# Keys of a prompt turned by VectorE in blocks of 32 and stored from SBUF, buffers released at the last scores, output units 512 columns wide

## The chip, the cores and the metric

The kernel runs on one core of a Trainium2 chip. The metric is the device time of one execution in microseconds (us): the median of three runs was 294.86 us (294.21 to 295.25). The engines named below are PE (TensorE, matmuls), DVE (VectorE), ACT (ScalarE), POOL (GpSimd) and SP (SyncE, which issues nearly all transfers). SBUF is the on-chip memory in 128 partitions, PSUM the accumulators that PE writes, in eight banks of 128 x 512 floats. A DMA moves data between the chip's DRAM and SBUF.

## The reference

One decoder layer is computed for two groups: a prompt of 512 tokens and 8 decode tokens, each with its own past. All data is float32.

```
h = x @ w_in                      # (512 + 8) x 1024 by 1024 x 3600
qa, ka, va, za, ga, qb, kb, vb, gb = split(h)
o_a = gated linear attention(qa, ka, va, gate(za)), 4 heads, chunked, RMS-normalised
o_b = dilated attention(qb, kb, vb), 8 heads of 64; three patterns of distances, one merged softmax
mix = [o_a * silu(ga), o_b * silu(gb)]
y   = LayerNorm(2**0.25 * x + mix @ w_out)       # 1024 x 1024
outputs: y for both groups, the states of the linear attention,
         the keys kb and values vb of both groups, token by token
```

For this change one output matters most: `k_win_prompt`, the keys of the prompt, 512 tokens x 512 features (1 MB), with one row per token.

## The kernel before

**Layout.** The input x is held transposed (features on partitions, tokens on the free axis). A projection in the feature-major form (`feature`) multiplies a weight tile of 128 columns with x and yields 128 features on partitions and the tokens on the free axis, in two units: 264 columns (256 prompt tokens and the 8 decode tokens) and 256 columns. Every unit accumulates over 8 pieces of the contraction (KT = 8), and each piece takes three matmuls, because weights and x are each split into a high and a low part in the fast float32 format (`fp32r`): high x high, high x low, low x high. So a unit has 24 matmuls. Splitting is one copy on ACT (the high part) and one subtraction on DVE (the low part).

**Keys.** `kb` comes in four groups of 128 features (m = 0 to 3), each in two units (u = 0, 1). Its evacuation (`parts`) writes the high part on ACT and the low part on DVE into `kp{m}`, which the scores use. The output wants token-major keys. Before, `keys_token_major` does it at the very end: for each of four token tiles eight matmuls against an identity turn the high and low parts and add them in PSUM, ACT copies the result into SBUF (`keys_out`, line 1024), and a 256 KB store leaves, the first from SP and three from ACT. These copies wait for `rstd3`, a step of the last normalisation.

**Output projection.** `out_first` computes the first 256 tokens and the decode tokens in feature-major units (g, f) of 264 columns; each is turned back by PE (`out_turn`). `out_unit` then computes the token tiles t = 2 and 3 token-major, in units of 24 matmuls with 256 output columns: `wo` holds four groups of 256 columns. `out_evac` adds the unit to the residual rows `y{t}` on DVE and gathers the statistics of the LayerNorm; `norm(t)` finishes a tile and stores it, in two halves for t = 3.

**Order.** The order of the work is found by a planner when the program is built (`Plan`, lines 189 to 358). Each task is a generator with a priority. The planner models when each engine is free and when operands are ready, and takes the operation that can start first, the lower priority number first among equals. `At(name, n)` holds a task back until a mark was set n times in this planning; it is no wait on the chip. `Need(tag, ...)` takes a buffer slot from a pool and holds the task back while none is free; `free` returns it, after as many calls as `share` asked for. On the chip each engine executes its list in order and waits only where data or buffer reuse demand it. So SP, whose transfers have one queue, issues in the planned order, as early as the slots allow.

**Pools.** "g" has 27 slots of 4 KB per partition (projections, keys, queries, gates, mix tiles, output rows), "w" 6 for split weights, "r" 2 for raw weights, "t1" 4 and "t2" 3 for small things. Split pieces of w_out may also use slots of "sv", "pt" and "g" (`Group.part`). PSUM banks are "d" (3, projections), "s" (3) and "t" (2). Before, `weighted` returns the query tiles `qh`, `ql` after the last weighted sum of a half (line 1194), and the key tiles `kp` after the turns at the end (line 1198).

**The decode path.** The eight decode tokens have their own chain: POOL multiplies past keys with the queries, DVE reduces, a softmax follows, then POOL and DVE do the same with past values. Its results enter the first output units through `mix_sample`.

Of the kernel before, what the change touches and what calls it, by code (L numbers as in the profile page):

```python
# [75 lines left out]
class Op:  # L76
# [3 lines left out]
    def __init__(self, eng, fn, args, kw):  # L80
# [13 lines left out]
        if fn == "dma_start":  # L94
            c = 640 if eng.name == "SP" else 100
            x = aps[aps[0].tensor.space == bass.MemoryType.DRAM]
            run = 4 * min(run_of(x) for x in aps)

            rate = 175 if x.ap[0][1] <= 64 else 340 if run >= 4096 else 230
            self.xfer = max(4 * total(x) / rate, 200)  # L100
            self.late = 600 * (rate == 175)
        elif eng.name == "PE":
            m, n, slow = size(aps[1]), size(aps[2]), aps[2].dtype == F32

            self.mode = tuple(32 if x <= 32 else 64 if x <= 64 else P for x in (aps[1].ap[0][1], m if slow and fn != "transpose" else P))
# [83 lines left out]
class Plan:  # L189
# [18 lines left out]
    def mark(self, name):  # L208
        self.marks[name] += 1
# [152 lines left out]
def trunk(ctx: ExitStack, tc: tile.TileContext, xT, xp, xs, state, ck, cv, w_in, wab, gnorm,  # L362
# [54 lines left out]
    rb = cst("rb", [66, NB, HB], F32R)  # L417
    ident_r = cst("ident_r", [P, P], F32R)
    ka_s, qa_s = cst("ka_s", [P, 2, NB]), cst("qa_s", [P, 2, NB])
# [25 lines left out]
    class Group:  # L445


        def __init__(self, src, c0, name, width):
            self.src, self.c0, self.name, self.w = src, c0, name, width
            self.parts = 1 if width == P else 2  # L450
            self.kk = KT // self.parts
            self.hi, self.lo, self.tiles = [], [], []

        def load(self, i):
# [13 lines left out]
        def split(self, i, raw):  # L468
            a = yield from self.part(f"hi{i}_")
            b = yield from self.part(f"lo{i}_")  # L470
            self.tiles.append((a, b))
            n = self.kk // self.parts
# [16 lines left out]
    groups = {f"{n}{i}": w_group(n, i, w) for n, c, w in names for i in range(c)}  # L489
    wo = [Group(w_out, g * GW, f"wo{g}_", GW) for g in range(4)]  # L490
    order = [g for k, g in groups.items() if k != "ka0"] + wo
# [89 lines left out]
    def fills():  # L581
        yield V.memset(rb.bitcast(F32)[64:66], 1.0)
        yield At("const")
        yield S.copy(ident_r, ident)
        mark("ident_r")
        raw = B["rb_raw"]
# [29 lines left out]
    def token(g, evac_f, evac):  # L616

        for f in range(2):
            fs = slice(f * P, f * P + P)
            ps = yield bank("d", f"ps_{g.name}f{f}")  # L620
            for k in range(KT):
                yield At(g.name, k // 2 + 1)
                h, l = xh[k][:, TS[0]], xl[k][:, TS[0]]
# [11 lines left out]
    def turn(ps):  # L635
# [5 lines left out]
        for t in range(2):  # L641
            yield T.transpose(o[:, t * P:t * P + P], f[:, t * P:t * P + P], ident)
        free(f)
        return o

# [20 lines left out]
    def dense():  # L666
# [29 lines left out]
        for x in ("qh0", "ql0", "qh1", "ql1"):  # L696
            yield from make(x, Need("g", x, [P, 4, 256], F32R))
        for i in range(4):
            yield from feature(groups[f"qb{i}"], parts("q", q_s, i, 0.125))
        for i in range(4):  # L700
            yield from make(f"kp{i}", Need("g", f"kp{i}", [P, 2, 512], F32R))
            yield from feature(groups[f"kb{i}"], parts("k", k_s, i, 1.0))
# [19 lines left out]
        for x in units[3:]:  # L722
            yield from out_first(x)
        for t in range(2, 4):
            for g in range(4):
                yield from out_unit(t, g)
        for t in range(TT):
            yield from keys_token_major(t)

# [267 lines left out]
    def parts(n, own, m, scale):  # L997

        def evac(ps, u):
# [6 lines left out]
            if u == 0:  # L1006
                yield S.mul(own[:, m, :], ps[:, 256:TW[0]], scale)
            free(ps)
            mark(f"{n}b{m}{u}")
            mark(f"{n}b")  # L1010
        return evac

    def keys_token_major(t):
        for m in range(4):
            yield At(f"kb{m}{t // 2}")
        yield At("ident_r")
        ps = yield bank(("d", "s", "t"), "ps_kw")
        for m in range(4):
            for x in range(2):
                yield T.matmul(ps[:, m * P:m * P + P], B[f"kp{m}"][:, x, t * P:t * P + P], ident_r, start=x == 0, stop=x == 1)  # L1020
        mark("kw")
        add(keys_out(t, ps), 11)

    def keys_out(t, ps):
        yield At("rstd3")
        kw = yield Need("t2" if t % 2 else "st", "kw", [P, 512])
        yield S.copy(kw, ps)
        free(ps)
        yield (S if t else D).dma_start(kw_p[t * P:t * P + P, :], kw)
        free(kw)  # L1030

# [8 lines left out]
    def va_into(i):  # L1040
        def evac_f(ps, f):
            c = slice(i * GW + f * P, i * GW + f * P + P)
            yield copy(vat[:, 2 * i + f, :], ps[:, GW:TW[0]])
            mark("vat")
            ps = yield from turn(ps)
            yield copy(B["va0"][:, :, c], ps[:, :GW].rearrange("p (t c) -> p t c", t=2))
# [9 lines left out]
    def vb_into(i):  # L1056
# [4 lines left out]
        def evac_f(ps, f):  # L1061
            c = slice(i * GW + f * P, i * GW + f * P + P)
            yield copy(vnt[:, 2 * i + f, :], ps[:, GW:TW[0]])
            mark("vnt")
            ps = yield from turn(ps)
# [34 lines left out]
    def scores(m, pi, qt):  # L1100
# [12 lines left out]
        for u in range(pi + 1):  # L1113
# [54 lines left out]
    def weighted(h, pi):  # L1168
# [280 lines left out]

    def out_unit(t, g):  # L1450
        u, tl = t // 2, slice((t % 2) * P, (t % 2) * P + P)
        ps = yield bank("d", f"ps_y{t}{g}")
        for k in range(KT):
            yield At(wo[g].name, k // 2 + 1)
            yield At(f"mix_a{u}", t % 2 + 1) if k < 4 else At(f"mix_b{u}{k - 4}")
            mh, ml = (B[f"m{x}{'ab'[k // 4]}{u}"][:, k % 4, tl] for x in "hl")
            hi, lo = wo[g].hi[k], wo[g].lo[k]
            yield from three(ps[:, :GW], k, ((mh, hi), (mh, lo), (ml, hi)))
        add(out_evac(t, g, ps[:, :GW]), 2)

# [11 lines left out]
    def out_half(g, f, ps, ks):  # L1472
        fs = slice(f * P, f * P + P)
        for k in ks:
            yield At(wo[g].name, k // 2 + 1)
# [3 lines left out]
            hi, lo = wo[g].hi[k][:, fs], wo[g].lo[k][:, fs]  # L1479
            yield from three(ps[:, :TW[0]], k, ((hi, mh), (lo, mh), (hi, ml)))  # L1480
# [20 lines left out]
    def out_evac(t, g, ps):  # L1501
        yield At(f"y{t}")
        y, st = B["y", t], B["stats", t]
        c = slice(g * GW, g * GW + GW)
        yield V.scalar_tensor_tensor(y[:, c], y[:, c], ALPHA, ps, op0=ALU.mult, op1=ALU.add)
        free(ps)
        yield V.bn_stats(st[:, g, :], y[:, c])
        mark(f"y{t}_done")
        if plan.marks[f"y{t}_done"] == 4:
# [79 lines left out]
    add(mix_sample(), 16)  # L1589
    add(ln_rows(), 17)  # L1590
    for pi in range(2):
        for n in "ab":
# [106 lines left out]
```

## Time and profile before

| | |
|---|---|
| median of the runs | 294.86 us (294.21 to 295.25) |
| profiled execution, its own time | 296.48 us |
| span of the profiled execution | 294.7 us |
| PE busy | 282.2 us |
| DVE busy | 229.3 us |
| ACT busy | 165.3 us |
| DMA queue of SP, share of 16 engines | 60.1% |

The page gives for each engine its busy time in the span; a busy PE is a PE with a matmul under way, not one at its peak. A row of a timeline begins with the start and the duration in us; "x2" are two instructions merged, and a bracket at the end names idle time before it and what ended it. A row of the table by stages covers the window that it names. The line number L357 is that of a helper through which all instructions are issued, so groups are told apart by the names of their tiles. `ps_kb` are banks of the key projection, `ps_yf` those of the feature-major and `ps_y` those of the token-major output units, `ps_kw` those of the key turns.

### The profile page before, as it was taken

What the parts mean: (1) busy time and instruction counts of PE and PEld (TensorE: products, weight loads), DVE (VectorE), ACT (ScalarE), POOL (GpSimd) and SP (SyncE); (2) the same over time, 40 slices, a digit from 0 to 9 for tenths busy, and PEclk for the clock granted to TensorE, in tenths of its full rate; (3) what the DMA queues carried; (4) which work ended last, traced back from release to release, by engine and by line L of the source; (5) the groups of instructions that cost most, each with busy time, mean ns of one, the idle gap of its engine ahead of it and who ended that gap; (6) DMA issues with size and microseconds to landing.
All of it is one profiled execution on the core that took longest, in us unless ns stands there. A gap on an engine that the chain in (4) does not pass through costs nothing.

```text
span 294.7 us, 7011 instructions
## 1 busy us (share of the span) xinstructions
PE 282.2 (96%) x2696; PEld 268.5 (91%) x2696; DVE 229.3 (78%) x566; ACT 165.3 (56%) x454; POOL 55.6 (19%) x73
## 2 busy tenths in 40 slices
PE   6989999999999999899999999999999999999992
PEld 2979999998999999889899899998999999999992
DVE  3858377998879877887889976989889965349944
ACT  4768325554676757267659672769769854111003
POOL 3000000000195354300241449030320000000000
PEclk9999999999999999999999999999999999999996
DMA  7946432222887695635999989654964788100315
GB/s 189 325 119 202 125 98 73 76 71 76 246 316 222 177 308 186 177 97 155 268 207 181 218 211 285 166 143 144 281 166 137 233 274 318 40 0 27 122 73 214
DMA packets 54107, 51.20 MB, mean 174 GB/s; under 512 B 4116, under 2 KB 46904, under 8 KB 54074
## 3 DMA queue, kind: packets, MB, share of 16 engines
q1 hardware_dynamic: 53642, 49.97, 60.1%
q10 hardware_dynamic: 432, 0.79, 0.7%
q8 instruction: 21, 0.34, 0.5%
q14 instruction: 12, 0.10, 0.1%
HBM read 45.19 MB, written 6.03 MB: 174 GB/s over the span
## 4 chain that ended last, share of the span: by engine, by line
PE 23%; DVE 17%; DMA 7%; ACT 4%; issue 2%; POOL 1%; SPq 0%; DVEq 0%; POOLq 0%; ACTq 0%
PE ps_yf L357 8%; PE ps_y L357 8%; DMA pb<-psd_s 3%; DVE o_pv L357 2%; PE ps_va_f L357 2%; DVE oa L357 2%; ACT sg L357 2%; DVE gb L357 1%; DMA out_dram<-vb_raw 1%; DMA raw_gb__2786<-in_w_in_dram 1%; PE ps_va L357 1%; PE ps_pv L357 1%; DVE ga L357 1%; DMA s<-in_state_dram 1%; DVE y L357 1%
## 5 line engine op out<-in xcount | busy, mean ns | idle before, releaser
L357 POOL TENSOR_TENSOR vv<-vv,pb 128x256 f32<-128x256 f32 x32 | 26.2, 853 | 68.7 <-DMA pb<-psd_s 31.3
L357 POOL TENSOR_TENSOR past<-past,qbc 128x256 f32<-128x256 f32 x32 | 25.4, 827 | 42.0 <-DMA past<-in_ck_dram 39.1
L357 ACT ACTIVATE pr<-pr,ms 128x128 f32<-128x128 f32 (+3 forms) x43 | 23.2, 554 | 8.8 <-DVE ms L357 8.8
L357 PE MATMUL ps_pt<-cf,pr 128*128 128x128 f32 x80 | 14.0, 276 | 0.8 <-DVE pt L357 0.8
L357 DVE CUSTOM_DVE_ANT_0 pr<-ps_s,strip 128x128 f32<-128x128 f32 (+3 forms) x32 | 14.3, 480 | 0.6 <-PE ps_vb_f L357 0.6
L357 ACT ACTIVATE sg<-sg 128x264 f32<-128x264 f32 (+1 forms) x32 | 13.3, 417 | 0.4
L357 ACT COPY feat_y<-ps_yf 128x256 f32<-128x256 f32 x8 | 3.0, 373 | 17.1 <-PE ps_yf L357 17.1
L357 DVE TENSOR_TENSOR ptl<-ps_pt,pth 128x384 fp32r<-128x384 f32 (+1 forms) x16 | 9.6, 617 | 1.8 <-ACT pth L357 1.7
L357 ACT ACTIVATE rstd<-mv 128x1 f32<-128x1 f32 x4 | 0.7, 203 | 17.8 <-DVE mv L357 17.8
L357 DVE TENSOR_REDUCE o_pv<-vv 128x4 f32<-128x1024 f32 x8 | 9.7, 1214 | 1.0 <-POOL vv L357 1.0
L357 PEld LDWEIGHTS ps_pt<-cf,pr 128*128 128x128 f32 x80 | 9.2, 141 | 1.3 <-PE ps_vb_f L357 1.0
L357 POOL MEMSET att<- 64x512 f32 x2 | 1.0, 522 | 48.5 <-DVE ks L357 48.5
L357 ACT ACTIVATE sq<-oa 128x128 f32<-128x128 f32 x16 | 4.8, 301 | 9.3 <-DVE oa L357 9.1
L357 DVE TENSOR_REDUCE lt<-past 128x16 f32<-128x1024 f32 x8 | 9.6, 1204 | 0.0
L357 ACT CAST pth<-ps_pt 128x384 fp32r<-128x384 f32 (+1 forms) x16 | 8.3, 533 | 2.3 <-PE ps_pt L357 2.0
L357 DVE COPY lt<-ps_yf 128x8 f32<-128x8 f32 x6 | 1.0, 167 | 10.9 <-ACT feat_y L357 10.9
L357 ACT ACTIVATE d<-d 128x512 f32<-128x512 f32 x13 | 7.7, 637 | 3.0 <-DVE d L357 3.0
L357 DVE TENSOR_SCALAR pr<-pr,ms 128x256 f32<-128x256 f32 (+3 forms) x21 | 8.7, 428 | 0.2
L357 ACT CAST pt<-ps_pt 128x128 fp32r<-128x128 f32 (+1 forms) x16 | 5.1, 321 | 6.6 <-PE ps_pt L357 6.5
L357 ACT COPY pvl<-ps_pv 64x256 f32<-64x256 f32 x16 | 5.8, 370 | 5.3 <-PE ps_pv L357 3.2
L357 DVE TENSOR_TENSOR d<-b 128x1024 f32<-128x1024 f32 x7 | 8.5, 1219 | 0.0
L357 DVE TENSOR_TENSOR obT<-ps_pv,pvl 64x256 f32<-64x256 f32 x16 | 6.7, 416 | 2.4 <-ACT pvl L357 2.1
(551 smaller groups left out, 1155.4 us busy)
## 6 DMA issues: line engine op xcount, KB each, us to landing
past<-in_ck_dram SPq DMA_DIRECT2D x8, 512.0 KB
vv<-in_cv_dram SPq DMA_DIRECT2D x8, 512.0 KB
pb<-psd_s SPq DMA_DIRECT2D x16, 256.0 KB
qbc<-qsd SPq DMA_DIRECT2D x8, 256.0 KB
strip<-tabr SPq DMA_DIRECT2D x8, 256.0 KB
y<-in_xp_dram SPq DMA_DIRECT2D x4, 512.0 KB
x_raw<-in_xT_dram SPq DMA_DIRECT2D x7, 260.0 KB
out_dram<-y SPq DMA_DIRECT2D x3, 512.0 KB
```

The lines of the kernel that those rows point to most:

```text
L357: getattr(eng.eng, op.fn)(*op.args, **op.kw)
```

## The change

Keys: `keys_out` is now part of the evacuation of a key unit. After the high and low parts, DVE's 32x32 block transpose reads the unit's 256 columns out of PSUM and writes them to `kw{m // 2}`, a tile of pool "g"; only then is the bank returned. In each block of 32 x 32 tokens and features are swapped, so partition 32a + i holds token 32b + i and, at columns 32b to 32b + 31, the features 32a to 32a + 31. A new task `keys_store` (priority 17.5) issues 16 stores from SP once all turns are planned and the first output tile has its first evacuation: each takes 32 partitions and one m, 64 KB in runs of 32 floats. The matmuls against the identity, the identity in `fp32r`, the four copies and the four stores at the end are gone.

Buffers: `scores` returns `kp` and the two query tiles itself; queries are shared by four calls, keys by two.

Output: `wo` is two groups of 512 columns, each loaded in four pieces of two k (before: four groups in two pieces of four k), with one mark per k (`Group.at`). Token tile 2 has two units of 512 columns, tile 3 one of 512 and two of 256. The feature-major units pick their 128 columns out of the wider group.

Values: `turn` no longer returns its buffer; the turned values `vb` are copied back into it before their store.

```diff
-            rate = 175 if x.ap[0][1] <= 64 else 340 if run >= 4096 else 230
+            rate = 60 if run <= 128 else 175 if x.ap[0][1] <= 64 else 340 if run >= 4096 else 230
...
-    ident_r = cst("ident_r", [P, P], F32R)
...
-            self.parts = 1 if width == P else 2
+            self.parts = width // P
             self.kk = KT // self.parts
+            self.n = KT if width == P else 512 // width
...
+        def at(self, k):
+            return At(self.name, k // self.n + 1)
...
-    wo = [Group(w_out, g * GW, f"wo{g}_", GW) for g in range(4)]
+    wo = [Group(w_out, g * 512, f"wo{g}_", 512) for g in range(2)]
...
         for x in ("qh0", "ql0", "qh1", "ql1"):
-            yield from make(x, Need("g", x, [P, 4, 256], F32R))
+            yield from make(x, Need("g", x, [P, 4, 256], F32R), 4)
...
-            yield from make(f"kp{i}", Need("g", f"kp{i}", [P, 2, 512], F32R))
+            yield from make(f"kp{i}", Need("g", f"kp{i}", [P, 2, 512], F32R), 2)
...
-        for t in range(2, 4):
-            for g in range(4):
-                yield from out_unit(t, g)
-        for t in range(TT):
-            yield from keys_token_major(t)
+        for t, c, w in ((2, 0, 512), (2, 512, 512), (3, 0, 512), (3, 512, GW), (3, 768, GW)):
+            yield from out_unit(t, c, w)
...
+            if n == "k":
+                add(keys_out(ps, m, u), 2)
+            else:
+                free(ps)
...
-    def keys_token_major(t):
-        for m in range(4):
-            yield At(f"kb{m}{t // 2}")
-        yield At("ident_r")
-        ps = yield bank(("d", "s", "t"), "ps_kw")
-        for m in range(4):
-            for x in range(2):
-                yield T.matmul(ps[:, m * P:m * P + P], B[f"kp{m}"][:, x, t * P:t * P + P], ident_r, start=x == 0, stop=x == 1)
-        mark("kw")
-        add(keys_out(t, ps), 11)
-
-    def keys_out(t, ps):
-        yield At("rstd3")
-        kw = yield Need("t2" if t % 2 else "st", "kw", [P, 512])
-        yield S.copy(kw, ps)
-        free(ps)
-        yield (S if t else D).dma_start(kw_p[t * P:t * P + P, :], kw)
-        free(kw)
+    def keys_out(ps, m, u):
+        if m % 2 + u == 0:
+            yield from make(f"kw{m // 2}", Need("g", f"kw{m // 2}", [P, 2, NP]))
+        yield At(f"kw{m // 2}")
+        yield V.transpose(B[f"kw{m // 2}"][:, m % 2, u * 256:u * 256 + 256], ps[:, :256])
+        free(ps)
+        mark("kw")
+
+    def keys_store():
+        yield At("kw", 8)
+        yield At("y0_done", 1)
+        for i in range(2):
+            kw = B[f"kw{i}"].rearrange("p m (b j) -> p m b j", j=32)
+            for m in range(2):
+                for a in range(4):
+                    c = (2 * i + m) * P + a * 32
+                    yield D.dma_start(kw_p[:, c:c + 32].rearrange("(b i) j -> i b j", i=32), kw[a * 32:a * 32 + 32, m])
+            free(B[f"kw{i}"])
...
-            raw = yield Need("t1", "vb_raw", [P, GW])
             yield copy(raw, ps[:, :GW])
...
+        free(kp, *qx)
...
-            free(B[f"qh{pi}"], B[f"ql{pi}"])
             if pi:
                 free(*(B[f"vhl{i}{u}"] for i in range(2) for u in range(2)))
-                yield At("kw", TT)
-                free(*(B[f"kp{m}"] for m in range(4)))
...
-    def out_unit(t, g):
+    def out_unit(t, c, w):
...
-            yield from three(ps[:, :GW], k, ((mh, hi), (mh, lo), (ml, hi)))
+            hi, lo = g.hi[k][:, cs], g.lo[k][:, cs]
+            yield from three(ps[:, :w], k, ((mh, hi), (mh, lo), (ml, hi)))
...
+    add(keys_store(), 17.5)
```

More of the change, by code (lines that the diff above doesn't have):

```diff
@@ L471, in split @@
             self.tiles.append((a, b))
-            n = self.kk // self.parts
+            n = self.n
             for k in range(0, self.kk, n):
@@ L583, in fills @@
         yield At("const")
-        yield S.copy(ident_r, ident)
-        mark("ident_r")
         raw = B["rb_raw"]
@@ L621, in token @@
             for k in range(KT):
-                yield At(g.name, k // 2 + 1)
+                yield g.at(k)
                 h, l = xh[k][:, TS[0]], xl[k][:, TS[0]]
@@ L642, in turn @@
             yield T.transpose(o[:, t * P:t * P + P], f[:, t * P:t * P + P], ident)
-        free(f)
-        return o
+        return o, f
     def sample_rows(x, rows):
@@ L1007, in evac @@
                 yield S.mul(own[:, m, :], ps[:, 256:TW[0]], scale)
-            free(ps)
             mark(f"{n}b{m}{u}")
             mark(f"{n}b")
-        return evac
-    def keys_token_major(t):
-        for m in range(4):
-            yield At(f"kb{m}{t // 2}")
-        yield At("ident_r")
-        ps = yield bank(("d", "s", "t"), "ps_kw")
-        for m in range(4):
-            for x in range(2):
-                yield T.matmul(ps[:, m * P:m * P + P], B[f"kp{m}"][:, x, t * P:t * P + P], ident_r, start=x == 0, stop=x == 1)
-        mark("kw")
-        add(keys_out(t, ps), 11)
-    def keys_out(t, ps):
-        yield At("rstd3")
-        kw = yield Need("t2" if t % 2 else "st", "kw", [P, 512])
-        yield S.copy(kw, ps)
-        free(ps)
-        yield (S if t else D).dma_start(kw_p[t * P:t * P + P, :], kw)
-        free(kw)
+            if n == "k":
+                add(keys_out(ps, m, u), 2)
+            else:
+                free(ps)
+        return evac
+    def keys_out(ps, m, u):
[4 more added lines that the diff above has]
+        free(ps)
+        mark("kw")
+    def keys_store():
[8 more added lines that the diff above has]
+            free(B[f"kw{i}"])
     def sample_v(x, n, out):
@@ L1044, in evac_f @@
             mark("vat")
-            ps = yield from turn(ps)
+            ps, f_t = yield from turn(ps)
+            free(f_t)
             yield copy(B["va0"][:, :, c], ps[:, :GW].rearrange("p (t c) -> p t c", t=2))
@@ L1064, in evac_f @@
             mark("vnt")
-            ps = yield from turn(ps)
+            ps, raw = yield from turn(ps)
             yield from parts_of(B[f"vhl{i}0"][:, :, 2 * f:2 * f + 2], ps[:, :GW].rearrange("p (t h d) -> p t h d", t=2, d=64))
             mark(f"vb{i}0")
-            raw = yield Need("t1", "vb_raw", [P, GW])
             yield copy(raw, ps[:, :GW])
@@ L1448, in residual @@
         mark(f"y{t}")
-    def out_unit(t, g):
-        u, tl = t // 2, slice((t % 2) * P, (t % 2) * P + P)
-        ps = yield bank("d", f"ps_y{t}{g}")
+    def out_unit(t, c, w):
+        u, tl, cs = t // 2, slice((t % 2) * P, (t % 2) * P + P), slice(c % 512, c % 512 + w)
+        g = wo[c // 512]
+        ps = yield bank("d", f"ps_y{t}{c // GW}")
         for k in range(KT):
-            yield At(wo[g].name, k // 2 + 1)
+            yield g.at(k)
             yield At(f"mix_a{u}", t % 2 + 1) if k < 4 else At(f"mix_b{u}{k - 4}")
             mh, ml = (B[f"m{x}{'ab'[k // 4]}{u}"][:, k % 4, tl] for x in "hl")
-            hi, lo = wo[g].hi[k], wo[g].lo[k]
-            yield from three(ps[:, :GW], k, ((mh, hi), (mh, lo), (ml, hi)))
-        add(out_evac(t, g, ps[:, :GW]), 2)
+            hi, lo = g.hi[k][:, cs], g.lo[k][:, cs]
+            yield from three(ps[:, :w], k, ((mh, hi), (mh, lo), (ml, hi)))
+        add(out_evac(t, c // GW, ps[:, :w]), 2)
     def out_first(*units):
@@ L1472, in out_half @@
     def out_half(g, f, ps, ks):
-        fs = slice(f * P, f * P + P)
+        w, c = wo[g // 2], g % 2 * GW + f * P
         for k in ks:
-            yield At(wo[g].name, k // 2 + 1)
+            yield w.at(k)
             yield At("mix_a0", 2) if k < 4 else At(f"mix_b0{k - 4}")
@@ L1478, in out_half @@
             mh, ml = (B[f"m{x}{'ab'[k // 4]}0"][:, k % 4, :] for x in "hl")
-            hi, lo = wo[g].hi[k][:, fs], wo[g].lo[k][:, fs]
+            hi, lo = w.hi[k][:, c:c + P], w.lo[k][:, c:c + P]
             yield from three(ps[:, :TW[0]], k, ((hi, mh), (lo, mh), (hi, ml)))
@@ L1503, in out_evac @@
         y, st = B["y", t], B["stats", t]
-        c = slice(g * GW, g * GW + GW)
+        c = slice(g * GW, g * GW + size(ps))
         yield V.scalar_tensor_tensor(y[:, c], y[:, c], ALPHA, ps, op0=ALU.mult, op1=ALU.add)
         free(ps)
-        yield V.bn_stats(st[:, g, :], y[:, c])
-        mark(f"y{t}_done")
+        for i in range(g, g + size(ps) // GW):
+            yield V.bn_stats(st[:, i, :], y[:, i * GW:i * GW + GW])
+            mark(f"y{t}_done")
         if plan.marks[f"y{t}_done"] == 4:
```

## The prediction

> **What bounds the kernel now.** I read the page's busy times first, then what TensorE (PE) waited for, then a table of windows cut at the stages, and last the end of the chain of waits.
>
> ```profile
> span 294.7 us, 7011 instructions
> PE 282.2 (96%) x2696; PEld 268.5 (91%) x2696; DVE 229.3 (78%) x566; ACT 165.3 (56%) x454; POOL 55.6 (19%) x73
> ...
> PE ps_yf L357 <- ACT mha L357: 0.3, 1, 0.3
> ...
> 75.00:102.00 27.00, 27.00 (x239) 25.88 (x240) 23.12 (x74) 18.53 (x60) 15.47 (x20) 1.00 0.78 247
> 102.00:116.00 14.00, 13.63 (x117) 13.43 (x116) 10.37 (x32) 8.03 (x27) 5.65 (x8) 1.00 0.85 262
> 116.00:136.00 20.00, 18.65 (x153) 17.02 (x152) 16.52 (x44) 11.42 (x36) 4.29 (x4) 1.00 0.43 126
> ...
> 190.00:210.00 20.00, 19.02 (x157) 18.63 (x156) 18.09 (x54) 14.66 (x52) 2.84 (x4) 1.00 0.63 165
> ...
> 236.70:262.10 25.40, 25.37 (x208) 25.23 (x209) 11.78 (x32) 8.35 (x22) 0.00 (x0) 1.00 0.47 170
> 262.10:285.80 23.70, 23.70 (x201) 23.40 (x200) 18.16 (x55) 2.15 (x11) 0.00 (x0) 1.00 0.18 69
> 285.80:294.70 8.90, 3.67 (x34) 3.53 (x32) 4.64 (x12) 2.44 (x6) 0.00 (x0) 0.75 0.47 177
> ```
>
> In a window's row stand its length, then the busy us of PE, of weight loads, VectorE (DVE), ScalarE (ACT) and GpSimd, then clock, DMA share and GB/s. PE is busy all through 75 to 102 us and through the output projection (236.7 to 285.8), at full clock. Elsewhere its idle time is small: 1.35 us in 116 to 136, 0.98 us in 190 to 210. So time is won in three ways only: less PE work, less PE idling, or a shorter end after PE's last unit. The last one is the chain's end:
>
> ```profile
> 236.73 7.56 PE ps_yf L357 x58
> ...
> 262.10 0.94 PE ps_y L357 x8
> ...
> 270.13 15.84 PE ps_y L357 x132
> 285.99 0.43 DVE y L357
> ...
> 290.15 0.75 DVE y L357
> ```
>
> The feature-major units (ps_yf) run from 236.73, the token-major ones (ps_y) from 262.10. DVE ends at 290.90, the span at 294.7: 3.8 us belong to the last store and the closing.
>
> **The change part by part. The end.** The 32 matmuls that turn the keys run after PE's last output unit, and the four stores of keys leave beside those of y.
>
> ```profile
> 285.67 0.28 PE L357 MATMUL ps_y<-hi_wo__3805,mlb 128*128 128x256 f32 x1
> 285.79 3.68 PE L357 MATMUL ps_kw<-ident_r,kp 128*128 128x128 f32 x32
> ...
> 290.93 0.33 SPq L357 DMA_DIRECT2D out_dram<-y  x1
> ...
> 292.50:293.00 0.50, 0.00 (x0) 0.00 (x0) 0.00 (x0) 0.00 (x0) 0.00 (x0) 0.50 0.98 365
> 293.00:293.50 0.50, 0.00 (x0) 0.00 (x0) 0.00 (x0) 0.00 (x0) 0.00 (x0) 0.50 0.63 234
> ...
> 279.99 0.33 SPq L357 DMA_DIRECT2D out_dram<-y  x1
> ...
> 280.40:280.90 0.50, 0.50 (x6) 0.50 (x5) 0.47 (x2) 0.00 (x0) 0.00 (x0) 1.00 0.35 123
> ...
> 281.90:282.40 0.50, 0.50 (x7) 0.50 (x6) 0.00 (x0) 0.00 (x0) 0.00 (x0) 1.00 0.41 164
> ```
>
> The 3.68 us of PE and the four ACT copies lie beside the last normalisation on DVE, which needs neither: worth nothing. The DMA engines are not free, though: 98% busy up to 293.0 and done at about 293.3. Of the six transfers of 256 KB (128 x 512 x 4 bytes) in this stretch, four are keys. With them gone, the last half of y, issued at 290.93, runs alone. The store of twice its size issued at 279.99 began to move about 0.7 us later (35% of the window's half us) and moved for 1.4 us, so this half takes about 0.7 + 0.7 us and ends near 292.4. Gain 0.9 us; bounds 0 (the closing waits for something else) and 1.6 (it starts as soon as it is issued).
>
> **Output units.** For row tiles 2 and 3, 8 units of 24 matmuls with 256 columns become 3 units with 512 and 2 with 256: 144 narrow matmuls turn into 72 wide ones, 48 stay. The last unit of before (first matmul here, last one and its successor above):
>
> ```profile
> 282.94 0.28 PE L357 MATMUL ps_y<-hi_wo__3715,mha 128*128 128x256 f32 x1
> ...
> 162.66 0.62 PE L357 MATMUL ps_s<-kp,qh 64*128 64x384 f32 x4
> ...
> 163.29 0.62 PE L357 MATMUL ps_s<-kp,qh 64*128 64x512 f32 x4
> ...
> 164.08 0.44 PE L357 MATMUL ps_turn<-cf,feat 128*128 128x128 f32 x2
> ```
>
> 24 starts in 2.85 us (282.94 to 285.79) are 118.8 ns for 256 columns. What a column costs shows in the scores, where six matmuls (the four shown and two with ql) run as three pairs: 0.63 us with 384 columns (162.66 to 163.29), 0.79 with 512 (163.29 to 164.08), hence 0.16 / 3 / 128 = 0.417 ns. So 106.7 of the 118.8 ns are columns and 12.1 are per matmul; 512 columns take about 225.5 ns. Gain 72 x 12.1 ns = 0.87 us, all on PE's full stretch, so on the path. Bounds 0 (the fixed part doubles with the width) and 0.87. [...]
>
> w_out still comes in 8 loads and 16 splits. What shifts is which unit needs which: the fifth feature-major unit now needs all four loads (eight splits) of the second half, in order of k. It starts at 249.39; at 0.12 us a matmul its 19th, k = 6, falls near 251.6, while the last split ends by 250.03.
>
> ```profile
> 248.74 1.29 DVE L357 TENSOR_TENSOR lo_wo__3806<-raw_wo__3718,hi_wo__3805 128x512 fp32r<-128x512 f32 x2
> ...
> 249.39 0.29 PE L357 MATMUL ps_yf<-mha,hi_wo__3580 128*128 128x264 f32 x1
> ```
>
> That costs nothing with 1.5 us to spare. Fewer evacuations save DVE three starts, off the path: the last unit stays 256 wide.
>
> **Key turns on DVE.** Eight transposes of 128x256 out of PSUM join the key evacuations. The nearest row, a DVE copy of that shape out of PSUM, takes 0.414 us, so 3.3 us in all. The key's own subtraction takes 0.412, a copy that selects 0.73 (8 x 0.73 = 5.8 us as the upper end).
>
> ```profile
> L357 DVE COPY feat<-ps_va_f x1: 414/414/414, 169.0 to 169.0; 128x256 f32<-128x256 f32 x1
> ...
> L357 DVE SCALAR_TENSOR_TENSOR kp<-ps_kb,kp x8: 406/412/428, 74.8 to 101.7; 128x256 fp32r<-128x256 f32 x8
> ...
> 70.12 0.73 DVE L357 COPY_PREDICATED near<-cm,ps_l 128x256 f32<-128x256 uint8 x1
> ```
>
> They fall into 75 to 102 us, where DVE has 27 - 23.1 = 3.9 us idle, and another 3.6 follow to 116. A PSUM bank of the keys stays taken 0.4 us longer; three banks and 2.8 us of matmuls per bank cover that. What is queued behind on DVE are softmax steps and the reductions of the decode logits, on which later loads wait. I take 0.2 us for what slips; between 0 and 3.3 (cover gone).
>
> **Buffers.** The pool "g" has 27 slots. Followed through the code's allocations, before has none left between the allocations of st_all and oa1, and again when the mix tiles are made. The new code holds two slots for the turned keys from the key stage on, but returns qh0 and ql0 with the scores of the first half, and four keys and two queries with the last scores; before, the queries stay until the last weighted sums and the keys until the turns at the end. So from the last scores (164 us) on, four slots more are free. DVE shows a place where that could count:
>
> ```profile
> 183.39 0.86 DVE L357 SCALAR_TENSOR_TENSOR oa<-va,dg,ps_oa 128x128 f32<-128x128 f32 x3 [2.49 <-PE ps_oa L357]
> ```
>
> PE's part in it is at most the 0.98 us of 190 to 210 and the 0.3 before ps_yf. I take 0.3 us; bounds 0 and 1.3. Earlier weight pieces mean the same DVE work earlier, so a loss is possible too (rival B). Reuse of the turned value's buffer, the dropped identity copy and the transfer rate in the planner's model move no work.
>
> **Key stores.** Sixteen DMAs of 512 runs of 128 bytes stand on SP's queue behind beta and ahead of the loads of y2 and y3.
>
> ```profile
> 242.57 0.38 SPq L357 DMA_DIRECT2D beta<-in_ln_b_dram  x1
> 243.04 1.06 SPq L357 DMA_DIRECT2D y<-in_xp_dram  x2
> ...
> 265.54 0.42 DVE L357 SCALAR_TENSOR_TENSOR y<-y,ps_y 128x256 f32<-128x256 f32 x1
> ...
> L357 SPq DMA_DIRECT2D strip<-tabr x16: 572/600/642, 73.6 to 154.8; - x16
> ...
> 251.00:252.00 1.00, 1.00 (x10) 1.00 (x10) 0.96 (x3) 0.00 (x0) 0.00 (x0) 1.00 0.43 168
> ...
> q1 hardware_dynamic: 752, 0.05, 139.8%
> ...
> q1 hardware_dynamic: 72, 0.03, 13.8%
> ```
>
> SP needs 16 x 0.6 = 9.6 us to issue them, idle time before. Packets: the first queue row covers 2.6 to 3.0 us, nearly all 64-byte loads (1.398 x 16 x 0.4 / 752 = 11.9 ns each on an engine), the second 276 to 277, the 512-byte store of the decode rows (0.138 x 16 / 72 = 30.7 ns). With 512 packets per engine that is 6.1 to 15.7 us; I take 15.7, being stores. The last loads of before, y2 and y3, ended at about 251.4; at the 365 GB/s seen above their 1 MB takes 2.9 us, so keys can run from 248.5 to 264.2 and y2 lands near 265.6. It is first needed when the first wide unit ends: 262.1 + 24 x 0.2255 = 267.5. Hidden by 1.9 us, cost 0.
>
> **Sum.** -0.9 - 0.87 + 0.2 - 0.3 = -1.87 us. The profiled execution took 296.48 us (span 294.7), 1.6 above the median of 294.86; it would come to 294.6 (span 292.8), the median to 293.0.
>
> **The rivals.** A, y2 comes late. If a 128-byte store costs more than (278.3 - 248.5 - 1.4) / 512 = 55 ns, y2 misses 278.3, when the fourth token-major unit (after three of 5.4 us) needs a bank that only y2's evacuation frees. PE then waits, and behind that evacuation DVE holds the normalisations of row tiles 0 and 1. At 61 ns, twice the store's row, y2 lands at 281.3: 3 us of PE and about 1 of DVE's backlog, near 297. For it: no run of 128 bytes is stored in this trace. Against: 64-byte loads at 11.9 ns. [...]
>
> B, slower through DVE: the 3.3 us don't fit, the decode chain slips, and the output projection starts later. Place: ps_yf's first matmul at 236.73, which waited for mha. Price up to 3.3 us, against the 1.77 us won at the units and the end: 294.86 + 3.3 - 1.77 = 296.4. It decides from a slip of 1.8 us on. For it: DVE is 90% busy from 190 to 210 and the scores and logits feed the decode path. Against: 7.5 us idle on DVE from 75 to 116.
>
> C, no difference: the fixed matmul cost grows with the width, the end keeps its length, and buffers bring nothing: 294.3 to 294.9.
>
> D, more: the free slots remove all of PE's 1.3 us: 294.86 - 1.77 - 1.3 = 291.8.
>
> **How the numbers follow.** Forecast 0.42 (293.0, own range 292.3 to 293.9), D 0.15, C 0.20, B 0.13, A 0.10. A measurement tells about 0.3%, 0.9 us, from no change: faster (below 293.98) 0.57, same 0.20, slower 0.23. The range runs from 291.5 (D, with some of the end's upper bound) to 296.4 (B), leaving out A.
>
> **What would show it.** Starts of 225 ns in the wide units; DMA idle by 292.5; transposes of 0.41 us with PE unbroken from 75 to 102; ps_yf at 236.4; key stores done by 265 and the first wide evacuation right behind its unit. It is wrong if PE idles near 278, or if ps_yf starts after 238.

## The result: 1.1% slower

The changed kernel takes 297.42 us (median of four runs, 296.83 to 299.5); the kernel before, beside it, 294.53 (293.34 to 295.25). The ratio is 1.011, with a 95% interval of 1.0066 to 1.0153. I had forecast 293.0 and "faster". A ratio leaves out executions that took over 1.5% longer than the fastest of their kernel (in e10_other_plan two of four), so it is not the quotient of the medians beside it; the two differ by up to 1%.

The profiled execution of the changed kernel took 297.63 us. First the page's totals, then the windows (columns as before: length, busy PE, weight loads, DVE, ACT, POOL, then clock, DMA share, GB/s).

```profile
span 295.8 us, 6803 instructions
...
PE 277.1 (94%) x2592; PEld 260.0 (88%) x2592; DVE 227.6 (77%) x560; ACT 168.4 (57%) x460; POOL 56.8 (19%) x73
```

```profile
75.00:102.00 27.00, 27.00 (x240) 26.05 (x241) 23.86 (x80) 18.11 (x61) 15.68 (x20) 1.00 0.81 247
...
116.00:136.00 20.00, 18.08 (x146) 16.62 (x147) 16.72 (x47) 13.65 (x39) 4.23 (x6) 1.00 0.42 131
...
150.00:170.00 20.00, 17.60 (x144) 15.82 (x141) 16.73 (x43) 15.04 (x37) 7.47 (x10) 1.00 0.94 179
170.00:190.00 20.00, 18.16 (x167) 17.06 (x167) 13.46 (x29) 8.08 (x29) 9.65 (x11) 1.00 0.83 217
...
240.00:264.40 24.40, 24.40 (x204) 24.40 (x203) 11.26 (x29) 7.84 (x21) 0.00 (x0) 1.00 0.84 225
264.40:288.20 23.80, 23.60 (x128) 19.57 (x126) 17.97 (x53) 2.12 (x11) 0.00 (x0) 1.00 0.18 70
```

Two windows of the kernel before that were not shown yet:

```profile
150.00:170.00 20.00, 19.69 (x164) 18.00 (x163) 19.03 (x48) 14.14 (x35) 6.67 (x8) 1.00 1.01 207
170.00:190.00 20.00, 20.00 (x193) 19.15 (x192) 15.21 (x40) 11.46 (x41) 9.74 (x12) 1.00 0.84 224
```

PE loses its time where the diff adds no work. From 150 to 190 us it idles 4.2 us (2.40 and 1.84), where it idled 0.3 before. From 75 to 102 us, where the added transposes run, and in the output projection it stands no more than before. The timeline of PE shows the new pauses (a bracket: idle before it, and what ended it) and the chain of waits the late start of the output projection:

```profile
117.46 0.33 PE L357 MATMUL ps_pt<-cf,pr 128*128 128x128 f32 x1 [1.70 <-DVE pt L357]
...
153.30 0.38 PE L357 MATMUL ps_va<-hi_va__1798,xx 128*128 128x256 f32 x1 [1.03 <-DVE ms L357]
...
165.29 0.44 PE L357 MATMUL ps_turn<-cf,feat 128*128 128x128 f32 x2 [0.91 <-ACT feat L357]
...
173.97 0.41 PE L357 MATMUL ps_turn<-cf,feat 128*128 128x128 f32 x2 [0.97 <-DVE ptl L357]
...
184.67 1.13 PE L357 MATMUL ps_oa<-va,att 128*128 128x128 f32 x8 [0.78 <-DVE st_all L357]
...
239.15 7.45 PE ps_yf L357 x58
```

These are softmax turns, value turns and the linear attention: other pauses than those of the kernel before, in an order of instructions that differs on all engines. The planner, given other buffers and other work, planned anew. That is the theory "order": the loss is the new order. Its rivals are "DVE" (the key transposes push back what is behind them) and "buffer" (a buffer held longer makes the chip wait).

### The profile page after: what moved, and what is told of

It is laid out like the page before. It is cut to its first block, busy times and chain, and to the rows that moved or that the text cites. A ratio compares the mean times of both kernels' runs of the same rounds, so it can differ in the third digit from the quotient of the medians.

```text
span 295.8 us, 6803 instructions
## 1 busy us (share of the span) xinstructions
PE 277.1 (94%) x2592; PEld 260.0 (88%) x2592; DVE 227.6 (77%) x560; ACT 168.4 (57%) x460; POOL 56.8 (19%) x73
## 4 chain that ended last, share of the span: by engine, by line
PE 67%; DVE 11%; DMA 9%; ACT 7%; POOL 2%; issue 2%; SPq 1%; POOLq 0%; DVEq 0%; ACTq 0%
PE ps_yf L357 8%; PE ps_qb L357 8%; PE ps_gb L357 8%; PE ps_y L357 8%; DMA pb<-psd_s 7%; PE ps_kb L357 7%; PE ps_qa L357 4%; PE ps_vb L357 4%; PE ps_ka L357 3%; PE ps_vb_f L357 3%; POOL vv L357 2%; PE ps_pv L357 2%; PE ps_ga L357 2%; ACT pr L357 2%; PE ps_s L357 2%
## 5 line engine op out<-in xcount | busy, mean ns | idle before, releaser
L357 POOL TENSOR_TENSOR vv<-vv,pb 128x256 f32<-128x256 f32 x32 | 27.5, 890 | 68.7 <-DMA pb<-psd_s 48.2
L357 ACT ACTIVATE pr<-pr,ms 128x128 f32<-128x128 f32 (+3 forms) x49 | 26.0, 547 | 7.4 <-DVE ms L357 7.1
L357 PE MATMUL ps_pt<-cf,pr 128*128 128x128 f32 x80 | 14.2, 277 | 2.7 <-DVE pt L357 1.7
L357 PE MATMUL ps_s<-kp,qh 64*128 64x128 f32 (+3 forms) x64 | 8.4, 345 | 0.0
L357 DVE TENSOR_TENSOR pt<-ps_pt,pt 128x128 fp32r<-128x128 f32 (+1 forms) x16 | 5.4, 347 | 3.5 <-ACT pt L357 3.5
```

The costliest lines, as they stand in the source:

```text
L357: getattr(eng.eng, op.fn)(*op.args, **op.kw)
```

## The experiments

Each ratio is the run's against executions of the kernel before on the same chip.

**Parts alone.** Three kernels are the kernel before with one part of the change: the output units (the hunks on `Group`, `wo`, `out_unit`, `out_half`, `out_evac`), the reuse of the value's buffer, or the early release of the queries:

```diff
 # e1_units
-        for t in range(2, 4):
-            for g in range(4):
-                yield from out_unit(t, g)
+        for t, c, w in ((2, 0, 512), (2, 512, 512), (3, 0, 512), (3, 512, GW), (3, 768, GW)):
+            yield from out_unit(t, c, w)
 # e2_turn
...
-            ps = yield from turn(ps)
+            ps, raw = yield from turn(ps)
...
-            raw = yield Need("t1", "vb_raw", [P, GW])
 # e3_release
...
+        free(*qx)
...
-            free(B[f"qh{pi}"], B[f"ql{pi}"])
```

> The kernel before with the 512-column output units and the regrouped w_out alone; keys, buffers and all the order up to the output projection stay. In the trace of the changed kernel the wide matmuls start 0.233 us apart, two narrow ones take 0.238, so 72 x 5 ns = 0.4 us are won. Theory 'order' (the loss lies ahead of the output projection, in the re-planned order): first output unit at 236.7 as before, time 0.3 to 0.5 us under before, about 294.1. Rival 'units' (the regrouped weights hold up the output projection): first output unit late, or gaps in it, time at or above before.

> The kernel before with the reuse of the turned value's buffer alone; no work is added or removed. Theory 'order': the planner takes another order from the first value store (about 105 us) on, and the first output unit starts 1 to 3 us later; time 295.5 to 297.5. Rival 'DVE' (the eight key transposes, 8 x 0.44 = 3.5 us, push the chain behind them back): they are absent here, so the time equals before, 294.5, within 0.5.

> The kernel before with the queries given up at their last scores, nothing else; no work is added or removed. Theory 'order': the planner takes another order from the linear attention's outputs (about 180 us) on; PE idles more in 180 to 236 us, time up to 2 us above before. Rival 'DVE': equal to before, within 0.5. My prediction had freed slots as a gain of 0.3 us: 294.2.

| run | median us | before | ratio | 95% interval |
|---|---|---|---|---|
| e1_units | 295.28 | 295.76 | 0.9955 | 0.9906 to 1.0004 |
| e2_turn | 296.95 | 295.76 | 1.0051 | 1.0004 to 1.0098 |
| e3_release | 301.71 | 295.76 | 1.0213 | 1.0161 to 1.0264 |

The units alone come out 0.5 us lower by the medians. The ratio would be 1.3 us, with an interval that takes in no gain at all, so the time neither shows nor contradicts the 0.4 us that the trace gives. Two edits that add no work at all cost 0.5% and 2.1%; giving the queries back earlier, which I had counted as a gain, is the dearest, 6 us where I had expected up to 2. In its trace (chain, ACT, PE, a window; this execution took 305.1 us, so the sizes are its own) the place is easy to read:

```profile
237.87 5.15 DMA raw_wo__3601<-in_w_out_dram
...
243.04 0.62 ACT L357 CAST hi_wo__3640<-raw_wo__3601 128x512 fp32r<-128x512 f32 x1
243.57 0.21 ACT L357 CAST mha<-ga_s 128x32 fp32r<-128x32 f32 x1
...
243.83 0.52 PE L357 MATMUL ps_yf<-mha,hi_wo__3367 128*128 128x264 f32 x1 [1.32 <-ACT mha L357]
...
244.00:248.00 4.00, 4.00 (x20) 3.72 (x21) 1.69 (x6) 1.49 (x4) 0.00 (x0) 0.58 0.81 256
```

In the new order the split of a w_out piece (243.04) stands on ACT ahead of the small cast (243.57) that the first output unit needs. The piece's load took 5.15 us, and the output projection began at 243.83 instead of 236.73.

**The old order, written out.** The next kernel has the whole change but the buffer reuse, with the order in which the kernel before takes its operations written into the code as a list and followed up to the first output unit. The key transposes go in where the planner finds DVE free; after the first output unit the planner is free again.

```diff
+            want = seq[-1] if seq else None
...
+                if want and t.label != want[0] and t.label.split(":")[0] not in ('keys_out',):
+                    continue
...
+            if want and t.label == want[0]:
+                op, ready = next(h for h in t.heads if h[0].eng.name == want[1])
+                seq.pop()
```

> The whole change but the reuse of the value's buffer, with the order of the kernel before written out and followed up to the first output unit (the key transposes are put in where DVE is free). DVE does all the added work of the changed kernel. Theory 'order': the first output unit starts at 236.7 to 237.4, the end is 0.9 shorter and the units 0.4, so 293.2 to 293.9. Rival 'DVE': the added 3.5 us of DVE still delay the first output unit by about 2.4, so 295.5 or more.

It took 295.06 us against 295.76: ratio 0.9962 (0.9909 to 1.0015). The added DVE work is all there (24.20 us of DVE from 75 to 102 us, 23.12 before), and the loss of 1.1% is not. PE stands 0.4 us in that window:

```profile
75.00:102.00 27.00, 26.61 (x235) 25.37 (x234) 24.20 (x78) 17.46 (x57) 15.09 (x20) 1.00 0.77 235
```

Later the same kernel was timed in twelve executions:

> The run with the old order in more rounds, beside the one without transposes. Theory: 1.3 us of gains less 0.4 to 1.0 us for the transposes (PE stood 0.4 us more from 75 to 102 us there), ratio 0.997 to 0.999, so faster than the changed kernel (1.011) by over 1%. Rival: the transposes cost 2 us or more here too and only the earlier rounds were lucky: ratio 1.002 or more.

295.89 against 295.40, ratio 1.0013 (0.9977 to 1.0049): between what the two theories gave, so neither is met to the letter. Both measurements together say: level with before.

**The new order without the new work.** The reverse: the work of the kernel before, with the early release of the queries and the reuse of the value's buffer, which the order needs, in the order of the changed kernel.

```diff
+ORDER = (...)    # the changed kernel's order, without keys_out
```

> The kernel before (keys turned by PE and stored at the end, narrow output units, no DVE transposes), its queries given up early and the value's buffer reused, and the order of the changed kernel written out and followed up to the first output unit. Theory 'order': it loses what the changed kernel loses and does not have its gains at the units (0.4) and the end (0.9): 298.5 to 299, first output unit at 238 to 240. Rival 'DVE': without the transposes the loss is gone: 294.5 to 295.5.

299.39 us against 295.68, ratio 1.0116 (1.0069 to 1.0164). No transposes, no key stores in the middle, narrow units, and the loss is there. This decides against "DVE" as the main cause. The windows of this run:

```profile
116.00:136.00 20.00, 17.55 (x133) 16.00 (x132) 15.71 (x46) 11.94 (x36) 5.56 (x7) 0.91 0.40 118
150.00:170.00 20.00, 18.95 (x156) 17.12 (x156) 16.99 (x42) 14.55 (x37) 6.80 (x9) 1.00 1.03 186
170.00:190.00 20.00, 19.22 (x174) 18.08 (x174) 14.61 (x29) 8.81 (x28) 10.62 (x12) 1.00 0.95 228
```

**The transposes by themselves.** In the changed kernel's order they are issued twice, or not at all; in the old order, not at all.

```diff
 # e7_twice
-        getattr(eng.eng, op.fn)(*op.args, **op.kw)
+        for _ in range(2 if op.fn == "transpose" and eng.name == "DVE" else 1):
+            getattr(eng.eng, op.fn)(*op.args, **op.kw)
 # e9_no_turns, e13_old_order_no_turns
+        if not (op.fn == "transpose" and eng.name == "DVE"):
+            getattr(eng.eng, op.fn)(*getattr(op, "real", op.args), **op.kw)
...
+                    op.real = (op.args[0], gw[a * 32:a * 32 + 32, m])    # gw: rows of gamma
```

> The changed kernel in its own order, each key transpose issued twice on the chip while the planner counts one: 8 x 0.44 = 3.5 us more of DVE in 74 to 101 us, nothing else. Rival 'DVE': if the first 3.5 us cost about 2.4 at the first output unit, the next cost as much or more, so 300 or above (changed kernel: 297.4). Theory 'order': they lie in DVE's idle time, at most 0.7 more, so 297.4 to 298.1.

> The changed kernel in its own order, with the eight key transposes counted by the planner but not issued; the 16 key stores read gamma's rows instead, so the prompt's keys are left out. Takes 8 x 0.44 = 3.5 us of DVE away and nothing else. Theory 'order': the transposes lie mostly beside other work, so 0 to 1 us under the changed kernel, 296.4 to 297.4, ratio to before 1.006 to 1.011. Rival 'DVE': they carry the loss (doubling them cost about 3 us), so about 3 us less, at or under before, ratio 0.999 or less.

> The run with the old order (the whole change but the buffer reuse), with the eight key transposes counted by the planner but not issued, the 16 key stores reading gamma's rows (the prompt's keys are left out). Theory: what is left are the gains, 0.4 us at the units and 0.9 at the end, so 1.3 us under before, ratio 0.9956; the difference to the run beside it is the transposes' cost in this order. Rival (the early release of queries and keys, or the 16 stores, also cost in the old order): ratio 0.998 or more.

| run | order | transposes | ratio | 95% interval |
|---|---|---|---|---|
| e9_no_turns | new | none | 1.0063 | 1.0002 to 1.0124 |
| changed kernel | new | one set | 1.011 | 1.0066 to 1.0153 |
| e7_twice | new | two sets | 1.0222 | 1.0156 to 1.0287 |
| e13_old_order_no_turns | old | none | 0.9964 | 0.993 to 0.9998 |
| e14_old_order_long | old | one set | 1.0013 | 0.9977 to 1.0049 |

One set costs 0.47% in the new order and 0.49% in the old one, 1.4 us each time. Neither difference is clear of zero by itself (at 95% they are good to about 0.75% and 0.5%), both together only just. As far as that goes, one set costs more than my 0.2 us, and less than half of the loss. The interval of e13_old_order_no_turns takes in its theory's 0.9956 and its rival's 0.998, so it does not decide between them.

The second set costs 3.3 us, good to about 2.3, nearly its whole 3.5. The 301.4 us of that run lie where the rival "DVE" had them, at 300 or above; "at most 0.7 more" was wrong, the cover from 75 to 116 us holds one set and not two. But with no set at all the new order still loses 0.6%, where that rival had no loss; the interval comes close to 1 there, and e8_new_order is the clearer case. PE's window with two sets, in which it stands 1.3 us that it does not with one:

```profile
75.00:102.00 27.00, 25.69 (x217) 23.68 (x218) 24.12 (x78) 16.35 (x56) 15.68 (x20) 1.00 0.69 221
```

**The held buffer.** The change's buffer reuse put back under the old order, and taken out of the changed kernel:

> As the run with the old order, and with the reuse of the turned value's buffer too: now the whole change, only the order of the kernel before. Theory 'order': as that run, so 0.5 to 1 us under before, if the reuse only acts through the planner's choice. Rival 'buffer' (the buffer is held from the turn through the value's store, so a later user of its pool waits for that store on the chip): one stall of 2 to 5 us at 105 to 120 us, first output unit at 239 to 242, time 2 to 4 us above that run.

> The changed kernel without the reuse of the turned value's buffer; the planner chooses its own order again. Theory 'order': still re-planned because of the releases and the key turns, so still slower than before, 296 to 302, with the first output unit at 238 or later. Theory 'buffer': the loss is gone, 293.2 to 294.5.

Under the old order: 301.6 against 295.68, ratio 1.017 (1.0065 to 1.0274), where the run without the reuse was level. DVE, PE and a window of this run:

```profile
115.17 0.28 DVE L402 TENSOR_TENSOR prod<-q_rows,k_rows 32x128 f32<-32x128 f32 x1 [6.90 <-DMA out_dram<-feat]
...
120.00:121.00 1.00, 0.92 (x4) 0.92 (x5) 0.99 (x3) 1.00 (x4) 1.00 (x2) 0.50 0.02 6
...
242.63 0.39 PE L402 MATMUL ps_yf<-mha,hi_wo__3346 128*128 128x264 f32 x1 [0.34 <-ACT mha L402]
```

DVE stands 6.9 us at `prod`, a decode step whose buffer in pool "t1" is the one that a value still leaves from: the reuse holds it from the turn to the end of the store. So "buffer" holds in the old order. It does not explain the changed kernel, whose planner knows of the held buffer and works around it. In its profile the longest wait for a value's store is this one of ACT, and PE is busy for 1.99 of the 2 us from 128 to 130:

```profile
129.42 0.26 ACT L357 COPY vnt_rows<-ps_rows 32x128 f32<-32x128 f32 x1 [1.62 <-DMA out_dram<-feat]
```

Taking the reuse out made the kernel slower, not faster, 300.34 against 295.68, ratio 1.0197 (1.0147 to 1.0247); that run is planned anew, so its order is another one again. In its profile PE stands 2.08 us before the output projection, which then runs at a clock of 0.50 from 238 to 240 us:

```profile
237.71 0.59 PE L357 MATMUL ps_yf<-mha,hi_wo__3348 128*128 128x264 f32 x1 [2.08 <-ACT mha L357]
...
238.00:240.00 2.00, 2.00 (x10) 2.00 (x11) 1.43 (x4) 0.97 (x3) 0.71 (x2) 0.50 0.85 282
```

**Any other order.** Is it this change, or any replanning? The kernel before, with one constant of the planner's model moved by 3%:

```diff
-TO_PE, FROM_PE, OTHER, AFTER_DMA, WITHIN = 600.0, 250.0, 150.0, 500.0, 120.0
+TO_PE, FROM_PE, OTHER, AFTER_DMA, WITHIN = 620.0, 250.0, 150.0, 500.0, 120.0    # e11: 580.0
```

> The kernel before with nothing changed but one constant of the planner's model (the time it assumes from another engine to PE, 620 instead of 600 ns): the same work in another order. Theory 'order', in its wide form (the order of before is a favourable one, nearly any other costs): 2 to 5 us above before, ratio 1.007 to 1.017. If the loss needs the freed or held buffers or the transposes: ratio 0.997 to 1.003.

> As the run with 620, with 580 ns: a third order of the same work. Theory 'order' in its wide form: ratio 1.005 to 1.017. If the loss needs the change's own parts: 0.997 to 1.003.

With 620: 313.92 against 295.44, ratio 1.0527 (1.0423 to 1.0631), more than I expected. With 580: 298.77, ratio 1.012 (1.0053 to 1.0187). Same work, same buffers, 1 to 5% lost. In the first of them (an execution of 315.1 us) PE's longest pauses, and what followed the second:

```profile
183.18 1.09 PE L357 MATMUL ps_pt<-cf,pr 128*128 128x128 f32 x4 [4.78 <-DVE pr L357]
...
257.12 0.59 PE L357 MATMUL ps_yf<-mhb,hi_wo__3411 128*128 128x264 f32 x1 [3.73 <-ACT mhb L357]
...
257.00:260.00 3.00, 2.88 (x13) 2.88 (x14) 0.19 (x1) 0.07 (x1) 0.00 (x0) 0.50 1.08 339
```

**The end by itself.** The kernel before without the loop over `keys_token_major`: it leaves out the turns and the stores of the prompt's keys.

> The kernel before without the turns and stores of the prompt's keys at its end (left out), its order unchanged up to there. Prices the end by itself: my prediction says 0.9 us less (bounds 0 and 1.6), the last store of y alone behind DVE; ratio about 0.997, and from the end of the last DVE instruction to the end of the span 2.9 us instead of 3.8.

294.27 against 295.44, ratio 0.998 (0.9903 to 1.0056): too wide for 0.9 us. The profile is sharper. DVE's last instruction ends at 293.39, the span at 296.3, 2.9 us later:

```profile
span 296.3 us, 6935 instructions
...
292.64 0.75 DVE L357 SCALAR_TENSOR_TENSOR y<-y,rstd,beta 128x512 f32<-128x512 f32 x1
```

**How far one profile can be trusted.** By the chains of waits the first output unit starts at 236.73 in the profile of before and at 239.15 in that of the changed kernel, which looks like the loss itself. But two kernels that keep the order of before up to there (e1, where I had expected 236.7, and e12) start it before and after both:

```profile
233.87 0.39 PE L357 MATMUL ps_yf<-mha,hi_wo__3405 128*128 128x264 f32 x1 [0.32 <-ACT mha L357]
...
239.23 0.40 PE L357 MATMUL ps_yf<-mha,hi_wo__3405 128*128 128x264 f32 x1 [0.33 <-ACT mha L357]
```

And the same kernel, profiled twice (e4, then e14), gave this:

```profile
L402 PE MATMUL ps_yf<-mha,hi_wo__3350 x8: 281/286/388, 236.6 to 246.5; 128*128 128x264 f32 x8
...
116.00:136.00 20.00, 19.76 (x164) 18.30 (x163) 16.59 (x47) 13.04 (x41) 2.90 (x4) 1.00 0.52 154
```

```profile
L402 PE MATMUL ps_yf<-mha,hi_wo__3350 x8: 279/285/390, 238.9 to 248.7; 128*128 128x264 f32 x8
...
116.00:136.00 20.00, 18.19 (x150) 16.64 (x149) 15.32 (x44) 11.45 (x37) 3.32 (x4) 1.00 0.42 127
```

So I compared PE's idle time in the three windows 116 to 136, 150 to 170 and 170 to 190 us over the profiles of each order. The old order: 1.7 (before), 1.0 (e1), 3.0 (e12), 1.1 (e4), 2.5 (e13), 3.0 us (e14). The new one: 6.2 (changed kernel), 5.3 (e7), 4.3 (e8), 4.5 us (e9). The means are 2.1 and 5.1, and the two ranges do not meet. The new order loses 3.0 us there, with or without transposes. The old order with the held buffer (e5) is in neither list: it stands 4.1 us in these windows, with its stall.

## Why the prediction was wrong

Put together from ratios (of 294.5 us): the order, that is e9 (1.0063) less the gains that e13 shows (0.9964), +1.0% or 2.9 us, good to about 2 us; one set of transposes +1.4 us, no better known; the gains at units and end -1.1 us, good to 1.0. The three come to the change's +3.2 by the way they are formed, so the sum confirms nothing. The run with the new order and none of the new work does: it gives 3.4 us for the order by another way, good to 1.4. The reuse of the buffer is in e9 and e8 and not in e13, so the order's term can hold some waiting for a value's store; in the profile of e9 PE stands 0.34 us at such a wait.

**The step that failed: buffers.** I followed the slots through the code and let them act on the old order, where they could only shorten waits: -0.3 us, bounds 0 and 1.3. The reuse of the value's buffer I put at nothing, as it moves no work. In place of that gain stands a new order that costs about 3 us. The releases, the reuse and the transposes all enter the planner, and each of them can make it choose another order; that of the kernel before is better than every other that was planned here. Alone, the release of the queries costs 2.1% and the reuse 0.5%. One pause points to the reuse: the wait for `pt` near 117 to 121 us, 1.70 us in the changed kernel and up to 2.04 in the other profiles of the new order, is also in that of the reuse alone, and without the reuse no wait for `pt` in that stretch is over 0.82 us:

```profile
120.69 0.33 PE L357 MATMUL ps_pt<-cf,pr 128*128 128x128 f32 x1 [1.67 <-DVE pt L357]
```

Which of the parts turns the changed kernel's order for the worse, and which single displaced instruction costs how much in it, stays open: with any part taken out, the planner plans anew, as the run without the reuse shows.

**Key turns: right in kind, too small as far as is known.** From the profile of the changed kernel:

```profile
L357 SPq DMA_DIRECT2D out_dram<-kw x16: 488/507/2698, 246.2 to 259.9; - x16
L357 DVE STREAM_TRANSPOSE kw<-ps_kb x8: 431/442/451, 73.9 to 100.2; 128x256 f32<-128x256 f32 x8
...
258.00:260.00 2.00, 2.00 (x19) 2.00 (x18) 0.52 (x3) 0.37 (x1) 0.00 (x0) 1.00 0.79 118
...
263.00:264.00 1.00, 1.00 (x10) 1.00 (x10) 0.00 (x0) 0.00 (x0) 0.00 (x0) 1.00 1.04 414
264.00:265.00 1.00, 1.00 (x7) 0.86 (x6) 0.04 (x1) 0.37 (x1) 0.00 (x0) 1.00 0.52 209
```

A transpose takes 0.442 us, where I took a copy's 0.414. PE stays unbroken from 75 to 102 us, as I said it would. But the term, 0.2 us, measures 1.4, good to 1.2 when both orders are taken together: within the bounds of 0 and 3.3, with 0.2 at the edge of what the runs allow.

**Key stores: right.** The loads of y2 and y3 end in the window at 264 to 265; I had 265.6 for y2, and nothing needs it before the first wide unit ends, near 269.9. Rival A falls. SP was held longer than I reckoned, 14.2 us for the 16 stores instead of 9.6, but little stands behind them. At 118 GB/s and a share of 0.79, a packet of 128 bytes costs an engine 128 / (118 / 16) x 0.79 = 13.7 ns; I had 11.9 to 30.7. The loads next to them moved 414 GB/s. What makes the stores slower, no run here shows.

**Output units: right in kind, half the size.** First wide start, fourteen intervals inside a unit, and the narrow end:

```profile
264.30 0.40 PE L357 MATMUL ps_y<-hi_wo__3371,mha 128*128 128x512 f32 x1
...
276.58 0.40 PE L357 MATMUL ps_y<-hi_wo__3371,mha 128*128 128x512 f32 x1
...
279.83 0.39 PE L357 MATMUL ps_y<-hi_wo__3493,mlb 128*128 128x512 f32 x1
```

3.25 us over 14 intervals are 232.1 ns. Against 118.8 ns for 256 columns that is 0.443 ns a column and 5.4 ns fixed. I had 0.417 and 12.1, taken from score matmuls of 64 rows that I counted in pairs (six with 384 columns in 0.63 us). So 72 x 5.4 ns = 0.39 us, not 0.87. The regrouped w_out cost nothing, as forecast: PE is busy for all 24.40 us of the window up to 264.4.

**The end: right.** From DVE's last instruction to the end of the span it is 2.9 us (292.94 to 295.8) instead of 3.8, and the DMA engines stop about where I put them, 1.5 us behind DVE:

```profile
292.19 0.75 DVE L357 SCALAR_TENSOR_TENSOR y<-y,rstd,beta 128x512 f32<-128x512 f32 x1
...
294.00:294.50 0.50, 0.00 (x0) 0.00 (x0) 0.00 (x0) 0.00 (x0) 0.00 (x0) 0.50 0.93 365
294.50:295.00 0.50, 0.00 (x0) 0.00 (x0) 0.00 (x0) 0.00 (x0) 0.00 (x0) 0.50 0.05 16
```

Rival B had the sign, and 0.13. Its place, a later start of the output projection, can't be told from single profiles, which spread as shown above; its mechanism, DVE's 3.3 us, accounts for about 1.4 of the loss. No rival said that the order itself would change for the worse.

The version closest to beating both kernels is the simplest: the wide units alone, 0.9955 with an interval that touches 1 (0.998 by the medians). It changes nothing ahead of the w_out loads. The whole change in the old order beats the changed kernel but is level with before.

## What to carry to other kernels

Where a planner or a scheduler orders the instructions, an edit costs what its work costs plus what the new order costs, and the second can be the larger: price it by planning the same work with a constant moved a little. To judge an edit, hold the order fixed and add the work; then replan. A freed buffer is a gain only if what it lets come earlier does not stand, on the same engine, ahead of something that is needed sooner: in the old order with the reuse, DVE did nothing of what stood behind `prod` while that waited 6.90 us.

## What I had not expected of the hardware

In some profiles PE had a lower clock after a pause. In the run with the buffer reuse alone, PE worked 0.44 of 2.6 us, and then got 0.57 of its clock for 4 us, by estimate worth another 4 x 0.43 = 1.7 us:

```profile
118.00:120.60 2.60, 0.44 (x2) 0.20 (x2) 2.57 (x6) 1.58 (x5) 2.39 (x4) 1.00 0.98 311
121.00:125.00 4.00, 4.00 (x23) 3.69 (x22) 1.99 (x6) 1.13 (x4) 0.00 (x0) 0.57 0.26 92
```

In the new order the window from 116 to 136 us ran at a mean clock of 0.91 in three of four profiles, an estimated 20 x 0.09 = 1.8 us that the idle times above leave out. The fourth, the changed kernel's own, has a pause of like length there (1.70 us, and 0.45 soon after) and full clock. The pause with full clock after it is the shortest of the four (the others 1.78 to 2.04 us). What decides whether a pause is followed by a lower clock, these profiles do not show.
